# A hybrid stick-breaking and convolution layer on one core: token layout, meta scores as wide products, and spaced steps for packed values

## The chip, the core and the metric

The kernel runs on one core of a Trainium2 chip. The metric is the device time of one execution, in microseconds (us), the median over several runs. The kernel before takes 1317.13 us, the median of 3 runs from 1316.32 to 1318.55.

## What is computed

One layer over a sequence of 2048 tokens of width 1024, with 16 learned meta tokens put in front and dropped at the end, all in float32:

```
u = rms_norm(h, pre_g)
glu_a, glu_b, conv_gate, q, k, v, sb_gate = split(u @ w_in)        # 7 x 512 columns

c = glu_a * sigmoid(glu_b)
c = silu(layer_norm(causal_depthwise_conv(c, width 31)))
c = (c @ w_pw2 + b_pw2) * silu(conv_gate)

z = q.k / sqrt(64), 8 heads of 64, keys strictly before the query   # stick-breaking
a[t,s] = sigmoid(z[t,s]) * prod over s < j < t of (1 - sigmoid(z[t,j]))
s = (a @ v) * silu(sb_gate)

h + rms_norm(concat[c, s] @ w_out, post_g)
```

## The kernel before

**Arithmetic.** Each float32 operand of a large product is split into a high and a low part (`split`, L462; `ev_qk`, L903) and the product is made as high x high + high x low + low x high, with tiles of 128 stationary columns and up to 512 moving ones. Attention uses differences of neighbouring values: the running products of (1 - beta) of a row of queries come from one DVE scan, are turned by PE (`flip`, L1341), split by ACT and DVE, and multiplied with the value differences (`gather`, L1358).

**Stages.** The sequence is cut into 4 chunks of 512 tokens (`TC`); chunk 0 also carries the meta tokens. The input projection of chunk 0 runs alone; after that `merge` weaves, for each chunk c, three streams: the attention of chunk c (`attention`, L1285), a filler (gates, the output projection of chunk c-1, the convolution's end, and the input projection of chunk c+1: `tail`), and `meta_keys` of chunk c-1 (L1503). An attention goes through units (head, key chunk); each unit weighs four blocks of 128 queries against 512 keys (`weigh`, L1301), and its results are turned and gathered later, `LAG` = 3 gathers behind.

**Order.** The order of all instructions is fixed when the program is built, by a planner: `Engine.issue` (L180) keeps a planned time for each engine from cost functions (`pe_cost`, L223, `dve_cost`, `act_cost`, `pool_cost`), `Later` (L143) holds small jobs with a due time until their inputs are ready by plan, and `merge` picks the stream whose next piece is ready, with `SHARES` (L77) saying how much filler work should be done at a given amount of attention work. On the chip each engine runs its list in order and waits on semaphores. SP issues most transfers, POOL some.

**PSUM.** Eight banks in four rings (`BANKS`, L51): two for the wide products ("mm"), four for everything that is turned or weighed ("T"), one for the attention's sums ("av"), one for the convolution ("cv"). A request for a T tile takes the oldest of the four and waits until its last reader is done.

**Tokens.** `load_first_in` (L653) brings chunk 0's tokens as eight tiles of 128 features x 512 tokens from `xturn`, which lies in memory as [128 features, 8 tiles, 512 tokens]. PE starts on a tile as soon as ACT and DVE have scaled and split it (`part_in`, L864). `load_later` (L777) brings the later chunks from `xlater`, two tiles at a time.

**Meta scores.** Every query also meets the 16 meta keys. `meta_scores` (L937) runs once for each chunk and each pair of heads: for each block of 128 queries it loads the queries as stationary operand and multiplies with `km`, high queries with 64 columns (high keys, low keys) and low queries with 32 (high keys). Two DVE operations add the parts into `sgm`, of which there are two, one per parity of the chunk; the second shares a tile with the constants and is called `cp` in the profile. `meta_keys` scans these scores with the products that the attention left in `cm`, turns the result with PE into one T bank, takes it up in four steps (ACT the high part, DVE the low part, POOL a copy), and makes one product per pair of heads with `vm`, the packed meta values. DVE adds the attention's sum to that product and multiplies with the gate; ACT and POOL split the result into `mixs` for the output projection.

**Values.** `values` (L1010) projects the values, POOL takes the differences of neighbours, and `turn` (L1042), a `Later` job, turns them with PE (tile `ev`), splits them and stores them for the attention.

## Time and profile before

| | us |
|---|---|
| median of 3 runs | 1317.13 |
| the profiled execution | 1318.35 |
| its span, first to last instruction | 1316.6 |
| PE busy | 1292.9 |
| DVE busy | 1023.1 |
| ACT busy | 734.8 |
| POOL busy | 674.9 |

PE (matmuls) is busy almost throughout; its weight loads (PEld) overlap the matmuls. Matmuls overlap each other too: one of 512 columns lasts 0.4 us from start to end, and the next starts 0.23 us after it. What an instruction takes from PE is therefore read from the starts in the order of time, not from the busy column. A wait is idle time in front of an instruction, put down to what ended it.

### The profile page before, as it was taken

Reading aid. Unit: us, or ns where it says so; the run is one execution under the profiler, and the core shown is the slowest. Engines: PE = TensorE matmul, PEld = TensorE weight load, DVE = VectorE, ACT = ScalarE, POOL = GpSimd, SP = SyncE. Lnnn points to the kernel's source line nnn. Section 1 sums busy time; section 2 is a strip of 40 time slices with the busy share of each in tenths; the row PEclk is TensorE's granted clock in tenths of the full one; section 3 lists DMA queues with packets and bytes.
Section 4 is the critical chain, followed back from the end, with each engine's and each line's share of the span. In section 5 each row is a group of like instructions: output and inputs, shape, how many; then the busy total and the mean of one; then the engine's idle time right before and its main releaser. Section 6 shows DMA issues by size and latency. Waiting matters only on the chain.

```text
span 1316.6 us, 22042 instructions
## 1 busy us (share of the span) xinstructions
PE 1292.9 (98%) x7522; PEld 1115.8 (85%) x7522; DVE 1023.1 (78%) x1470; ACT 734.8 (56%) x1461; POOL 674.9 (51%) x807
## 2 busy tenths in 40 slices
PE   8999999999999999999999999999999999999897
PEld 8998888887799878887789988888787889888797
DVE  5999889998884588984587478985448987899964
ACT  6544355344465452676555544588775665666543
POOL 2555578767677430788742231499787212322402
PEclk9999999999999999999999999999999999999999
DMA  6687787999878996676756696666667456676555
GB/s 230 217 266 234 240 274 258 304 342 321 267 241 269 314 299 196 204 233 215 229 180 193 188 342 198 195 193 215 200 185 231 137 156 191 193 250 217 177 160 184
DMA packets 166399, 300.82 MB, mean 228 GB/s; under 512 B 17280, under 2 KB 71744, under 8 KB 166288
## 3 DMA queue, kind: packets, MB, share of 16 engines
q1 hardware_dynamic: 152496, 251.44, 61.5%
q0 software_dynamic: 13792, 47.98, 9.5%
q8 instruction: 59, 0.97, 0.3%
q14 instruction: 52, 0.43, 0.1%
HBM read 221.90 MB, written 77.46 MB: 227 GB/s over the span
## 4 chain that ended last, share of the span: by engine, by line
PE 86%; DVE 6%; DMA 3%; ACT 2%; issue 1%; POOL 1%; SPq 0%; DVEq 0%; POOLq 0%; ACTq 0%
PE mm L218 56%; PE T L218 21%; PE av L218 9%; DVE pr L218 1%; DMA w<-wscr 1%; DMA ev<-x 1%; DVE ul L218 1%; DVE tok L218 1%; DVE cv L218 1%; DMA tok<-xlater 1%; POOL ev L218 1%; DVE mixs L218 1%; DMA pr<-xturn 0%; DVE al L218 0%; PE cv L218 0%
## 5 line engine op out<-in xcount | busy, mean ns | idle before, releaser
L218 PE MATMUL mm<-uh,w 128*128 128x512 f32 (+1 forms) x1936 | 566.9, 379 | 1.8 <-ACT uh L218 1.5
L218 PEld LDWEIGHTS mm<-uh,w 128*128 128x128 f32 x1936 | 338.7, 190 | 54.2 <-ACT uh L218 2.2
L218 PE MATMUL mm<-ul,w 128*128 128x512 f32 (+1 forms) x968 | 358.9, 372 | 0.0
L218 DVE TENSOR_TENSOR_SCAN pr<-T,pr,zcol 128x512 f32<-128x512 f32 x192 | 245.2, 1277 | 56.6 <-ACT T L218 54.0
L218 DVE TENSOR_TENSOR al<-T,ah 128x512 fp32r<-128x512 f32 (+1 forms) x320 | 191.3, 598 | 102.9 <-ACT ah L218 101.4
L218 ACT ACTIVATE ah<-T 128x512 fp32r<-128x512 f32 (+1 forms) x320 | 170.1, 532 | 156.1 <-PE T L218 155.0
L218 DVE SCALAR_TENSOR_TENSOR cv<-ct,cp,cv 128x512 f32<-128x512 f32 x319 | 238.9, 749 | 6.7
L218 ACT ACTIVATE T<-T 128x512 f32<-128x512 f32 (+2 forms) x320 | 167.5, 525 | 109.6 <-PE T L218 103.8
L218 POOL TENSOR_TENSOR acc<-acc,pd 128x512 f32<-128x512 f32 x150 | 194.7, 1298 | 41.3 <-ACT pd L218 34.6
L218 POOL TENSOR_TENSOR w<-wr,w 128x512 fp32r<-128x512 f32 x132 | 171.3, 1301 | 80.3 <-ACT w L218 79.4
L218 PEld LDWEIGHTS mm<-ul,w 128*128 128x128 f32 x968 | 183.0, 190 | 33.9 <-DVE ul L218 0.7
L218 PE MATMUL T<-kk,q 128*128 128x512 f32 (+3 forms) x640 | 191.8, 383 | 3.4 <-DVE mixs L218 1.1
L218 PE MATMUL T<-ident,pr 128*128 128x128 f32 x1088 | 171.4, 273 | 2.7 <-DVE al L218 1.7
L218 PEld LDWEIGHTS T<-ident,pr 128*128 128x128 f32 x1088 | 135.0, 140 | 35.6 <-DVE al L218 2.7
L218 DVE TENSOR_TENSOR_SCAN pr<-T,tri 128x128 f32<-128x128 f32 (+3 forms) x128 | 103.4, 814 | 28.0 <-ACT T L218 27.8
L218 PEld LDWEIGHTS T<-kk,q 128*128 128x128 f32 x640 | 105.6, 190 | 17.5 <-issue 1.5
L218 PE MATMUL av<-ah,vk 128*128 128x512 f32 (+1 forms) x320 | 119.5, 373 | 0.0
L218 ACT ACTIVATE pd<-ct,cp 128x512 f32<-128x512 f32 x150 | 106.7, 718 | 22.7 <-POOL acc L218 21.9
L218 PE MATMUL av<-al,vk 128*128 128x512 f32 (+1 forms) x320 | 117.2, 366 | 0.0
L218 ACT ACTIVATE w<-wr 128x512 fp32r<-128x512 f32 x140 | 86.9, 626 | 38.5 <-PE mm L218 11.8
L218 POOL COPY cm<-pr 128x1 f32<-128x1 f32 x120 | 23.9, 200 | 135.1 <-DVE pr L218 134.7
L218 PE MATMUL mm<-w,mixc 128*128 128x256 f32 x600 | 80.7, 283 | 0.3 <-ACT tok L218 0.3
(212 smaller groups left out, 1574.8 us busy)
## 6 DMA issues: line engine op xcount, KB each, us to landing
w<-wscr SPq DMA_DIRECT2D x150, 512.0 KB, 4.1
wr<-wpack SPq DMA_DIRECT2D x140, 256.0 KB, 4.5
wscr<-w POOLq DMA_DIRECT2D x68, 512.0 KB, 4.8
kk<-kscr SPq DMA_DIRECT2D x80, 256.0 KB, 4.5
vk<-vscr SPq DMA_DIRECT2D x80, 256.0 KB, 3.8
q<-qscr SPq DMA_DIRECT2D x64, 256.0 KB, 5.5
vscr<-mixs SPq DMA_DIRECT2D x32, 256.0 KB, 3.5
qscr<-ehl SPq DMA_DIRECT2D x32, 256.0 KB, 3.1
```

The costliest lines, as they stand in the source:

```text
L218: return call(out, *args, **kw)
```

## The change

- `xturn` is laid out tile by tile, [8 tiles, 128 features, 512 tokens], and `xlater` in pairs of tiles, [chunk, pair, feature, 2, tokens].
- `meta_scores` takes the keys as stationary operand: 64 columns (low keys beside high keys, then high keys beside zeros) against 512 moving queries, two products for each chunk and pair of heads. ACT copies one half of the result and DVE adds the other; the four pairs of heads lie in one tile `zt` of 128 partitions x 512 queries, which takes the second `sgm`'s place. In unit 2 of the chunk's attention PE turns `zt` in four transposes, and one DVE copy brings it into `sgm`, of which there is one.
- `turn` jobs get 2.0 us on their due time.
- In `meta_keys` each value product of the first kind (all heads of a chunk) is planned at least 1.8 us after the stream came to it, the sum goes from PSUM into `sr`, and the multiplication with the gate moves from DVE to POOL.
- In `attention` a block is always weighed before the next gather; before, the last gather of a diagonal unit went ahead.
- The planner's least price for a product rises from 0.06 to 0.11, and `SHARES` moves by 1.3 to 1.9.

```
-    [(28.1, 169.2)], [(71.5, 214.4)], [(114.3, 214.4)], [(123.8, 97.4), (158.7, 126.3)],
+    [(29.8, 169.2)], [(73.1, 214.4)], [(116.0, 214.4)], [(125.1, 97.4), (160.4, 126.3)],
...
-        return t
+        return t + self.late
...
-    return (0.108 if name == "transpose" else max(n * 4.537e-4, 0.06)), 0.19
+    return (0.108 if name == "transpose" else max(n * 4.537e-4, 0.11)), 0.19
...
-    both = const.tile([P, ncp + NTB * NH * MS], F32, name="cp")
-    cp = both[:, : ncp + KD * NM]
+    both = const.tile([P, ncp + TC], F32, name="cp")
+    cp, zt = both[:, : ncp + KD * NM], both[:, ncp:]
...
-    km = const.tile([P, 2, NJ, 2 * NM], F32R, name="km")
+    km = const.tile([P, NJ, 3, 2 * NM], F32R, name="km")
...
-            sp.dma_start(ts[k], xturn[:, k])
+            sp.dma_start(ts[k], xturn[k])
...
-            sp.dma_start(t[:, k : k + 2], xlater[c - 1, :, k0 : k0 + 2])
+            sp.dma_start(t[:, k : k + 2], xlater[c - 1, k0 // 2])
...
-    def meta_scores(c, j, hi, lo):
-
-        sg = sgm[c % 2]
-        if j == 0:
-            pool.memset(sg[:, :, :, NM:], 0.0)
-        pt = PT("T", [P, TC])[:, : NTB * 4 * NM].rearrange("p (b i s) -> p b i s", b=NTB, i=2)
-        for r in range(NTB):
-            ts = slice(NM + r * P, NM + (r + 1) * P)
-            pe.matmul(pt[:, r], hi[:, ts], km[:, :, j, :], start=(r == 0), stop=False)
+    def meta_scores(j, hi, lo):
+
+        pt = PT("T", [P, TC])
+        for i, t in ((0, hi), (1, lo)):
             pe.matmul(
-                pt[:, r, 0], lo[:, ts], km[:, 0, j, :], start=False, stop=(r == NTB - 1)
-            )
-        a, b = (pt[:, :, i].rearrange("p b (e s) -> p b e s", e=2) for i in range(2))
-        dve.tensor_copy(sg[:, :, 2 * j : 2 * j + 2, 0:NM], b)
-        dve.tensor_tensor(
-            sg[:, :, 2 * j : 2 * j + 2, 0:NM], a, sg[:, :, 2 * j : 2 * j + 2, 0:NM], op=ALU.add
-        )
-        if j == NJ - 1:
-            keep["sgm", c] = True
+                pt[: 4 * NM], km[:, j, i : i + 2].rearrange("p i s -> p (i s)"), t[:, NM:],
+                start=(i == 0), stop=(i == 1),
+            )
+        zj = zt[2 * j * NM : 2 * (j + 1) * NM]
+        act.activation(zj, pt[: 2 * NM], AF.Copy)
+        dve.tensor_tensor(zj, pt[2 * NM : 4 * NM], zj, op=ALU.add)
...
-                when(lambda: turn(dv, j, P, NM, NTB), [dv], [f"v{j}"], tag="T")
+                when(lambda: turn(dv, j, P, NM, NTB), [dv], [f"v{j}"], tag="T", late=2.0)
...
-                ready = len(pend) >= LAG
-                short = ready and pend[0][0]["diag"] and pend[0][1] == NTB - 1
-                for what in (1, 0) if short else (0, 1):
-                    if what == 0 and u:
-                        yield need(heads[u["h"]]["q2"], u["kk"], tag="T")
-                        weigh(u, b)
-                    if what and ready:
-                        yield needs_of(*pend[0])
-                        gather(*pend.pop(0))
+                if u:
+                    yield need(heads[u["h"]]["q2"], u["kk"], tag="T")
+                    weigh(u, b)
+                if len(pend) >= LAG:
+                    yield needs_of(*pend[0])
+                    gather(*pend.pop(0))
...
-            if i == 1:
+            if i == 2:
+                force(zt)
+                yield need(zt, tag="T")
+                pt = PT("T", [P, NTB, NH, NM])
+                for r in range(NTB):
+                    pe.transpose(
+                        pt[:, r].rearrange("p h s -> p (h s)"), zt[:, r * P : (r + 1) * P], ident
+                    )
+                dve.tensor_copy(sgm[:, :, :, 0:NM], pt)
+                pool.memset(sgm[:, :, :, NM:], 0.0)
+                keep["sgm", c] = True
...
-            yield need(m, vm, sr, gt, tag="T")
+            ready, t0 = need(m, vm, sr, gt, tag="T"), pe.now + 1.8
+            yield lambda: ready() if part else max(ready(), t0)
             pj = PT("T", [P, TC])
             pe.matmul(pj, vm[: 6 * NM, j], m[: 6 * NM], start=True, stop=True)
             hold.difference_update((sr.name, gt.name, m.name))
-            dve.tensor_tensor(pj, pj, sr, op=ALU.add)
-            dve.tensor_tensor(sr, pj, gt, op=ALU.mult)
+            dve.tensor_tensor(pj if part else sr, pj, sr, op=ALU.add)
+            (dve if part else pool).tensor_tensor(sr, pj if part else sr, gt, op=ALU.mult)
```

## Rows read from the trace of the kernel before

**Rows 1.** The page, part 1: busy time of each engine, its share of the span and its instructions.

```profile
PE 1292.9 (98%) x7522; PEld 1115.8 (85%) x7522; DVE 1023.1 (78%) x1470; ACT 734.8 (56%) x1461; POOL 674.9 (51%) x807
```

**Rows 2.** Stretches of the span: from and to, its length, then busy us (and instructions) of PE, PEld, DVE, ACT and POOL, the granted clock, the DMA engines' busy share and GB/s.

```profile
40.00:135.00 95.00, 93.79 (x680) 88.46 (x679) 88.35 (x138) 47.33 (x98) 49.61 (x51) 1.00 0.72 231
135.00:340.00 205.00, 204.27 (x998) 168.50 (x997) 188.06 (x289) 96.00 (x192) 145.61 (x189) 1.00 0.88 294
340.00:640.00 300.00, 296.75 (x1657) 253.47 (x1656) 206.85 (x300) 167.93 (x332) 181.02 (x205) 1.00 0.76 243
640.00:985.00 345.00, 342.65 (x1920) 291.04 (x1919) 242.83 (x329) 211.04 (x408) 188.60 (x206) 1.00 0.68 212
985.00:1230.00 245.00, 242.67 (x1490) 210.26 (x1489) 216.18 (x283) 151.88 (x313) 77.21 (x104) 0.99 0.64 199
1230.00:1250.00 20.00, 16.44 (x92) 12.96 (x91) 18.33 (x28) 11.42 (x22) 9.98 (x11) 0.91 0.43 143
```

**Rows 3.** Waits of PE, longest sum first: who waited for whom, us in total, times, the longest.

```profile
PE T L218 <- DVE mixs L218: 3.7, 3, 1.7
PE T L218 <- POOL ev L218: 2.2, 3, 1.3
```

**Rows 4.** The instructions that read the tile `km`: duration in ns (least, median, most), first and last start, forms (stationary, moving).

```profile
L218 PEld LDWEIGHTS T<-km,ehl x128: 186/192/192, 118.9 to 987.5; 128*128 128x128 f32 x128
L218 PE MATMUL T<-km,ehl x128: 192/263/298, 119.1 to 987.5; 128*128 128x64 f32 x64, 128*128 128x32 f32 x64
```

**Rows 5.** PE in order of time around the first group of meta scores: start, us to the end of the last, count, and idle time before it in brackets.

```profile
118.42 0.63 PE L218 MATMUL mm<-uh,w 128*128 128x512 f32 x2
118.88 0.40 PE L218 MATMUL mm<-ul,w 128*128 128x512 f32 x1
...
119.93 0.71 PE L218 MATMUL mm<-uh,w 128*128 128x512 f32 x2
```

**Rows 6.** PE in order of time: the turned weights of the first `meta_keys` and what follows, and where PE stops in each of the three stages.

```profile
346.31 0.60 PE L218 MATMUL T<-ident,ev 128*128 128x128 f32 x4
346.67 0.71 PE L218 MATMUL T<-kk,q 128*128 128x512 f32 x2
...
353.59 0.70 PE L218 MATMUL T<-kk,q 128*128 128x512 f32 x2 [1.14 <-DVE mixs L218]
...
654.16 0.52 PE L218 MATMUL T<-ident,pr 128*128 128x128 f32 x3 [0.86 <-DVE mixs L218]
...
1001.62 0.47 PE L218 MATMUL T<-mixs,vm 96*128 96x512 f32 x1 [1.73 <-DVE mixs L218]
```

**Rows 7.** Groups of instructions by line, engine, operation, tile and shape: busy us, mean ns of one, idle time before them and what ended it. The score operations, the four-step uptake of ACT and DVE, and the product with the gate on DVE beside the nearest one on POOL.

```profile
L218 DVE TENSOR_TENSOR sgm<-T,sgm 128x128 f32<-128x128 f32 x8 | 2.3, 292 | 0.3
...
L218 ACT ACTIVATE mixs<-T 32x512 fp32r<-32x512 f32 x12 | 7.1, 590 | 10.3 <-DVE mixs L218 9.2 <-PE T L218 1.1
...
L218 DVE TENSOR_TENSOR mixs<-T,mixs 32x512 fp32r<-32x512 f32 x12 | 8.2, 685 | 6.0 <-ACT mixs L218 5.9
...
L218 DVE TENSOR_TENSOR tok<-T,tok 128x512 f32<-128x512 f32 x12 | 8.3, 691 | 0.4
...
L218 POOL TENSOR_TENSOR mixs<-tok,mixs 128x512 fp32r<-128x512 f32 x12 | 15.4, 1289 | 1.0 <-ACT mixs L218 0.9
```

**Rows 8.** PE in order of time: the longest wait in front of a value turn.

```profile
601.17 0.66 PE L218 MATMUL T<-ident,ev 128*128 128x128 f32 x4 [1.25 <-POOL ev L218]
```

**Rows 9.** DVE in order of time: the first and the fourth of the four steps of the third stage.

```profile
996.76 0.68 DVE L218 TENSOR_TENSOR mixs<-T,mixs 32x512 fp32r<-32x512 f32 x1
...
1000.78 0.69 DVE L218 TENSOR_TENSOR mixs<-T,mixs 32x512 fp32r<-32x512 f32 x1 [0.66 <-ACT mixs L218]
```

**Rows 10.** Two stretches after the third stop, columns as in rows 2.

```profile
1000.00:1005.00 5.00, 2.91 (x10) 2.20 (x11) 3.83 (x7) 3.50 (x7) 4.16 (x6) 0.87 0.17 67
1005.00:1010.00 5.00, 5.00 (x19) 3.89 (x19) 4.86 (x9) 1.50 (x3) 4.98 (x6) 0.79 0.39 111
```

**Rows 11.** The scans over the tile `sgm`, columns as in rows 4.

```profile
L218 DVE TENSOR_TENSOR_SCAN sgm<-sgm,cm x8: 408/414/1465, 341.4 to 991.1; 128x136 f32<-128x136 f32 x8
```

**Rows 12.** The tile `mixs` from 356 to 382 us: output products, POOL's low parts, and the last three value products; columns as in rows 4.

```profile
L218 PE MATMUL mm<-w,mixs x12: 278/280/363, 380.0 to 381.4; 128*128 128x256 f32 x12
...
L218 POOL TENSOR_TENSOR mixs<-tok,mixs x4: 1287/1288/1307, 360.4 to 366.7; 128x512 fp32r<-128x512 f32 x4
...
L218 PE MATMUL T<-mixs,vm x3: 391/393/399, 357.2 to 359.0; 96*128 96x512 f32 x3
```

**Rows 13.** PE in order of time at the start: the two waits for tokens.

```profile
7.93 0.76 PE L218 MATMUL mm<-uh,w 128*128 128x264 f32 x4 [0.76 <-ACT uh L218]
...
9.96 0.92 PE L218 MATMUL mm<-uh,w 128*128 128x264 f32 x4 [0.73 <-ACT uh L218]
```

**Rows 14.** Stretches of the start, columns as in rows 2.

```profile
4.00:5.00 1.00, 1.00 (x6) 1.00 (x6) 0.63 (x3) 0.60 (x3) 0.00 (x0) 1.00 0.48 113
...
8.00:9.00 1.00, 0.97 (x6) 0.75 (x6) 0.82 (x2) 0.63 (x1) 0.00 (x0) 1.00 1.02 379
...
10.00:14.00 4.00, 4.00 (x19) 3.82 (x20) 4.00 (x7) 3.95 (x7) 0.00 (x0) 0.57 1.05 404
```

**Rows 15.** PE in order of time: the longest wait between 1230 and 1250 us.

```profile
1235.20 0.66 PE L218 MATMUL T<-ident,pr 128*128 128x128 f32 x4 [1.09 <-DVE al L218]
```

**Rows 16.** The sum over three stretches, 340 to 380, 640 to 690 and 985 to 1030 us, in which the meta values are made: their length and the busy us of each engine.

```profile
sum 135.00, PE 129.82 PEld 107.65 DVE 115.60 ACT 76.28 POOL 88.28; mean PE 43.27 PEld 35.88 DVE 38.53 ACT 25.43 POOL 29.43
```

More of the change, by code (lines that the diff above doesn't have):

```diff
@@ L141, with __init__ @@
     count = 0
-    def __init__(self, clock, what, ins, outs, engine, date, room):
+    def __init__(self, clock, what, ins, outs, engine, date, room, late):
         self.clock, self.what, self.ins, self.outs = clock, what, ins, outs
-        self.engine, self.date, self.room = engine, date, room
+        self.engine, self.date, self.room, self.late = engine, date, room, late
         Later.count += 1
@@ L282, in force, with when @@
             run(clock.writers(mark)[0])
-    def when(what, ins, outs=(), engine=None, date=0.0, tag=None):
-        soon.append(Later(clock, what, ins, outs, engine, date, tag))
+    def when(what, ins, outs=(), engine=None, date=0.0, tag=None, late=0.0):
+        soon.append(Later(clock, what, ins, outs, engine, date, tag, late))
     pe = Engine(clock, nc.tensor, pe_cost, 0.15, run)
@@ L385, in trunk @@
     vl = const.tile([P, 2, P], F32R, name="vl")
-    km = const.tile([P, 2, NJ, 2 * NM], F32R, name="km")
+    km = const.tile([P, NJ, 3, 2 * NM], F32R, name="km")
     cm = const.tile([P, NTB, NH, MS], F32, name="cm")
-    sgm = [
-        const.tile([P, NTB, NH, MS], F32, name="sgm"),
-        both[:, ncp:].rearrange("p (b h s) -> p b h s", b=NTB, h=NH),
-    ]
+    sgm = const.tile([P, NTB, NH, MS], F32, name="sgm")
     ct = [const.tile([P, HIST + TC], F32, name=f"ct{j}") for j in range(NJ)]
@@ L400, in clear @@
         nc.gpsimd.memset(cm, 0.0)
+        nc.gpsimd.memset(sgm, 0.0)
     kscr = dr.tile([NH, 2, HD, NM + SEQ], F32, name="kscr")
@@ L932, in qk_proj @@
                 when(
-                    lambda a=(c, j, hi, lo): meta_scores(*a), [hi, lo], [sgm[c % 2]], tag="T",
-                    date=pe.now + 3.0,
-                )
-    def meta_scores(c, j, hi, lo):
-        sg = sgm[c % 2]
-        if j == 0:
-            pool.memset(sg[:, :, :, NM:], 0.0)
-        pt = PT("T", [P, TC])[:, : NTB * 4 * NM].rearrange("p (b i s) -> p b i s", b=NTB, i=2)
-        for r in range(NTB):
-            ts = slice(NM + r * P, NM + (r + 1) * P)
-            pe.matmul(pt[:, r], hi[:, ts], km[:, :, j, :], start=(r == 0), stop=False)
+                    lambda a=(j, hi, lo): meta_scores(*a), [hi, lo], [zt], tag="T",
+                    date=pe.now + 4.0,
+                )
+    def meta_scores(j, hi, lo):
+        pt = PT("T", [P, TC])
+        for i, t in ((0, hi), (1, lo)):
             pe.matmul(
-                pt[:, r, 0], lo[:, ts], km[:, 0, j, :], start=False, stop=(r == NTB - 1)
-            )
-        a, b = (pt[:, :, i].rearrange("p b (e s) -> p b e s", e=2) for i in range(2))
-        dve.tensor_copy(sg[:, :, 2 * j : 2 * j + 2, 0:NM], b)
-        dve.tensor_tensor(
-            sg[:, :, 2 * j : 2 * j + 2, 0:NM], a, sg[:, :, 2 * j : 2 * j + 2, 0:NM], op=ALU.add
-        )
-        if j == NJ - 1:
-            keep["sgm", c] = True
+                pt[: 4 * NM], km[:, j, i : i + 2].rearrange("p i s -> p (i s)"), t[:, NM:],
+                start=(i == 0), stop=(i == 1),
+            )
+        zj = zt[2 * j * NM : 2 * (j + 1) * NM]
+        act.activation(zj, pt[: 2 * NM], AF.Copy)
+        dve.tensor_tensor(zj, pt[2 * NM : 4 * NM], zj, op=ALU.add)
     def in_proj(c):
@@ L1037, in differences @@
                 pool.tensor_copy(vcol[c % 2][:, j], vt[:, NM + P :: P])
-                when(lambda: turn(dv, j, P, NM, NTB), [dv], [f"v{j}"], tag="T")
+                when(lambda: turn(dv, j, P, NM, NTB), [dv], [f"v{j}"], tag="T", late=2.0)
                 if c == 0:
-                    when(lambda: turn(dv, j, NM, 0, 1), [dv], [f"v{j}"], tag="T")
+                    when(lambda: turn(dv, j, NM, 0, 1), [dv], [f"v{j}"], tag="T", late=2.0)
             def turn(dv, j, rows, t0, nb):
@@ L1075, in meta_k @@
                 sp.dma_start(
-                    km[rows, i, :, e * NM : (e + 1) * NM].bitcast(F32),
+                    km[rows, :, 1 - i, e * NM : (e + 1) * NM].bitcast(F32),
                     kscr[e::2, i, :, 0:NM].rearrange("j d s -> d j s"),
@@ L1326, in weigh @@
                 bm = keep["bm"][:, h - EARLY, r, h]
-                zm = sgm[c % 2][:, r, h, 0:NM]
+                zm = sgm[:, r, h, 0:NM]
                 when(
@@ L1522, in meta_keys @@
             dve.tensor_tensor_scan(
-                fl(sg), fl(sg), fl(cm), 0.0, op0=ALU.mult, op1=ALU.max
+                fl(sgm), fl(sgm), fl(cm), 0.0, op0=ALU.mult, op1=ALU.max
             )
-        when(lambda: pool.tensor_copy(bm[:, :, hs], zm), [sg], [bm])
+        when(lambda: pool.tensor_copy(bm[:, :, hs], zm), [sgm], [bm])
         given = {}
@@ L1927, in last_room @@
         pool.memset(a[:, 4:6], 0.0)
-        zm = sgm[c % 2][:, :, EARLY:, 0:NM]
+        zm = sgm[:, :, EARLY:, 0:NM]
         act.activation(zm, zm, AF.Sigmoid, scale=-SCALE)
@@ L2008 @@
         "xturn": np.ascontiguousarray(
-            f["x"][0, :TC].reshape(TC, KD, P).transpose(2, 1, 0)
+            f["x"][0, :TC].reshape(TC, KD, P).transpose(1, 2, 0)
         ),
         "xlater": np.ascontiguousarray(
-            f["x"][0, TC:].reshape(NCH - 1, TC, KD, P).transpose(0, 3, 2, 1)
+            f["x"][0, TC:].reshape(NCH - 1, TC, KD // 2, 2, P).transpose(0, 2, 4, 3, 1)
         ),
```

3 lines of the change are left out of this document (1 added, 2 removed).

## The prediction

> **What bounds the kernel now.** I read the page first: TensorE's matmul row is busy for 1292.9 of 1316.6 us [rows 1]. Then the same by stage [rows 2]: between 40 and 1230 us PE is idle for 1.21 + 0.73 + 3.25 + 2.35 + 2.33 = 9.9 us in all, and 3.6 more between 1230 and 1250; what is left lies at the start and the end. So in the body two things count: the matmuls that PE has to issue, and the few waits that make up the 9.9 us. Work that moves between the other engines counts only where PE ends up waiting for it. Last I read whom PE waits for [rows 3]: no wait is a habit; the longest sums are 2 to 4 us, in three places each.
>
> The profiled execution took 1318.35 us (its span is 1316.6), 1.2 us over the median of the three runs, 1317.13. I make the sum against 1318.35 and take the 1.2 us off at the end. A measurement of this kernel tells about 0.2% (2.6 us) from no change.
>
> **Part 1, the meta scores.** Now each of 16 (chunk, head pair) groups issues eight products, half of 64 and half of 32 columns, each with 128 queries loaded as the stationary operand [rows 4]. In the order of time [rows 5] the last full product before a group starts at 118.88 and the first after it at 119.93; a full 512-column product takes 0.23 (two in 0.46, from 118.42 to 118.88). So a group costs 1.05 - 0.23 = 0.82 us, and 16 cost 13.1. The busy column does not give this, since pipelined products overlap. After: two 512-column products per group, 16 x 2 x 0.23 = 7.4 us, and four transposes per chunk to turn the scores back. Four transposes take 0.36 (346.31 to 346.67 in [rows 6]), 4 x 0.36 = 1.4. Saving 13.1 - 8.8 = **4.3 us**. A stationary tile of 64 columns is in no row. One end: its load hides behind the product before, as loads here do, 4.3. Other end: the whole 0.19 of a load [rows 4] lies open 32 times, 6.1 us, and the part loses 1.8. I take the first: the nearest row, the product with 96 stationary rows, takes 0.39 from start to end [rows 12], as a full one does (0.40 in [rows 5]). Off PE, two DVE operations of 0.29 per group become one ACT copy (0.59) and one DVE add (0.69), priced by the 32x512 rows of [rows 7], plus one DVE copy of a bank per chunk, some 0.7: ACT +9.4 us, DVE +4.5 us over the run. The score bank is held some 0.7 us longer, and PE is who asks for the next one; but where the first groups lie PE goes on without a gap [rows 5], so I cost it at nothing. If that cover goes, it is 16 x 0.7 = 11 us at the very most. One score buffer replaces two; it is written in unit 2 of an attention, and the previous chunk's scores are read at that attention's beginning, so no wait.
>
> **Part 2, the delayed value turns.** `turn` gets 2.0 us more on the planner's date. Its transposes are what PE waits for at POOL: 2.2 us in 3 waits, none over 1.3 [rows 3], the longest at 601.17 [rows 8]. 2.0 covers the longest, so I take **2.2 us**. Bounds: 0 (POOL is late by something else in the new order) to 2.7 (each wait also loses the overlap of a product with the next, 0.40 - 0.23). The results go to memory and are read a stage later; nothing is late next.
>
> **Part 3, the spaced steps of the meta values.** PE stops in all three stages where they lie: 1.14 at 353.59, 0.86 at 654.16, 1.73 at 1001.62 [rows 6], and after the last the granted clock falls: 0.87 and 0.79 over 5 us each, with 2.4 GHz on one side and 1.2 on the other, 1.7 us of full speed [rows 10]. What it waits for is one PSUM bank. The transposed weights (346.31 in the first stage) are taken up from it in four steps, ACT then DVE, one after another: DVE starts its first at 996.76 and its fourth at 1000.78, a step every 1.34 us, done at 1001.47 [rows 9]. PE's fourth request for a T bank after the transposes comes round to this bank, and it stops until 0.15 us after that end. The change does not shorten this chain. It puts 1.8 us before each value product, so fewer requests fall into those 5 to 7 us; only in the third stage are two of the four requests value products. So I count half of that stage's 1.73 + 1.7: **1.5 us** (1.7 would be the half; some of the main stream moves up). Bounds: 2 us lost (the main stream asks earlier and stops longer) to 1.14 + 0.86 + 1.73 + 1.7 = 5.4 gained. The second multiplication moves from DVE (12 x 0.69) to POOL, where such a product takes 1.29 [rows 7]: 15.5 us more on POOL, 8.3 less on DVE. POOL then delivers the mixed values later, by the spaced steps (7.2 us for four; now the last three start within 1.8) and one or two queued products, some 6 us in all. In the first stage the last POOL product starts at 366.7 and takes 1.29, and the output products first read its kind at 380.0 [rows 12]. The 12 us between hide it.
>
> Here a rule speaks against the change. What the trace shows first: a DVE scan with two SBUF inputs takes 1.465 us at worst against 0.414 [rows 11]. The Trainium skill, "SBUF — State Buffer", section "SBUF: two separate sides", says that a DVE operation with two SBUF inputs and a GpSimd operation exclude each other for a whole instruction. By that rule the 12 moved products can stop 12 DVE operations; this is rival (d), worked out there from the rows.
>
> **Part 4, the token layout.** PE's first products wait for tokens: 0.76 and 0.73 [rows 13], and the clock falls behind that (0.57 from 10 to 14 us, 1.7 us of full speed). From 4 to 5 us the transfers move 113 GB/s, later 379 to 404 [rows 14]. If the slow stretch came from the 16 KB pitch of the tokens' rows, up to 0.76 + 0.73 + 1.7 = 3.2 us could go. But the same pitch is moving at 379 GB/s from 8 to 9 us, while tiles 2 and 3 come in. So I take **0.5**, bounds 0 to 3.2. The Trainium skill, "DMA: Bandwidth & Descriptors", section "Latency and other measured facts", lists row pitches at large powers of two as slow, from 512 KiB on, and advises contiguous tiles; by it the whole 3.2 would come and the sum would be 1305.9. The row at 8 us does not bear that out. The later tokens' transfers hide: PE's waits have none of them.
>
> **Part 5, the planner.** Its price for a short product rises from 0.06 to 0.11, the end of a diagonal is no longer gathered before the next unit is weighed, and the shares move by 1.7. This takes no instruction away, but all orders after about 110 us are dealt anew. Waits not named above are 9.9 - 2.2 - 3.7 = 4.0 us in the body and the 3.6 at 1230 to 1250, behind DVE like the 1.09 in [rows 15]. They may shrink by half or double in the body: I take 0, between -4 and +5.
>
> **Sum.** 4.3 + 2.2 + 1.5 + 0.5 = 8.5 us; 1318.35 - 8.5 = 1309.8, less 1.2 for the median: **1308.6 us**.
>
> **Rivals.** (a) *Only the instructions go.* The new order has as many waits as the old: 1317.1 - 4.3 = 1312.8. For it: the bank chain of part 3 is untouched. Against: the waits of part 2 have a known lateness. 22%. (b) *More heals*: the start (2.7 more) and half of the waits at 1230 to 1250 (1.8): about 1304. 11%. (c) *The 64-column load lies open*: 6.1 lost, 1314.7, so the scores do not gain what they should. Every load in these rows hides. 8%. (d) *Slower: POOL locks DVE out.* In the three stages of part 3 the moved products fall on DVE operations with two SBUF inputs; each stops one by 1.465 - 0.414 = 1.05 us, 12 x 1.05 = 12.6 us; if PE waits for all of them, 1308.6 + 12.6 = 1321. It decides once DVE runs out of slack there. It has 135.0 - 115.6 = 19 us in the three [rows 16], and the move frees 8.3 more, which speaks against it; for it, that PE's stops there are already behind DVE. 12%.
>
> **How the numbers follow.** The forecast has 47%, from 1305 to 1312. Below 1302 would need (b) and more; above 1317.5 lies most of (d) and little else. Both ends together leave out about 2 in 10, so the range is 1302 to 1317.5. Faster by over 0.2% (under 1314.5): the forecast's 47, 16 of (a), (b)'s 11 and 1 of (c), together 75. Slower by over 0.2% (over 1319.8): (d), 11 of its 12. Within 0.2%: 14, the rest of (a), (c) and (d).
>
> **What would show it.** Right: 32 products of 512 columns from the packed keys, 0.46 us per group; no PE wait for POOL's differences; the four-step chain still at 1.34 us a step, with PE's stop shorter or gone in the third stage; the start within 1 us of now. Wrong: start transfers at 350 GB/s from 4 us on and PE 2 to 3 us earlier (part 4 too low); stops behind T banks or DVE of over 10 us in the body (part 5); DVE scans of 1.4 us around the moved products (d); a gap at each 64-column load (c).

## The result and the profile after

The changed kernel takes **1310.43 us** (median of 4 runs, 1310.05 to 1311.82) against 1316.99 for the kernel before in the same session: ratio 0.995, 95% interval 0.9933 to 0.9968. The profiled execution took 1310.28 us, 8.07 less than the one before (1318.35), which lay 1.2 us above its median; by the medians the gain is 6.6 us.

The page's first part and the stages answer to [rows 1] and [rows 2].

```profile
PE 1284.4 (98%) x7442; PEld 1106.4 (85%) x7442; DVE 1019.2 (78%) x1446; ACT 743.0 (57%) x1477; POOL 690.4 (53%) x820
```

```profile
340.00:640.00 300.00, 296.11 (x1638) 252.12 (x1639) 207.50 (x298) 169.81 (x337) 189.67 (x213) 1.00 0.77 245
640.00:985.00 345.00, 343.97 (x1917) 292.13 (x1916) 244.43 (x326) 217.59 (x419) 200.30 (x215) 1.00 0.69 218
985.00:1230.00 245.00, 240.33 (x1480) 208.61 (x1480) 213.26 (x279) 149.07 (x307) 77.83 (x105) 0.99 0.63 195
```

PE is busy 8.5 us less, but it does not stand still less: between 340 and 1230 us it is idle for 3.89 + 1.03 + 4.67 = 9.6 us, against 7.9 in [rows 2]. The third stop of part 3 has moved from 1001 to 990 us; the stages are cut at fixed times, so work also moves across their edges.

The busy column overlaps products, so I also add up by starts. Each product gets a slot: 0.454 ns per moving column, at least 0.108 us, and 0.1085 for a transpose. The sum of the slots is PE's **work**; what the distance from one start to the next has beyond its slot is **excess** (waits, slow clock). In all kernels here work + excess + 10.4 to 11.1 us is the profiled time. Before: 1270.5 + 37.3. After: 1265.8 + 33.6. So 4.65 of the 8.07 us are fewer slots, and 3.7 are less excess. The slots are a model: from start to start, the 16 groups with their transposes take 4.2 us less. And one trace is one execution: beside run 1 the kernel before took from 1313.7 to 1322.4 us, so a us or two of excess between two traces is not yet a difference.

**The scores.** The products over the tile `km` [rows 4], and PE in order of time around one group [rows 5]:

```profile
L218 PEld LDWEIGHTS T<-ehl,km x32: 133/134/137, 117.2 to 978.2; 128*64 128x64 f32 x32
L218 PE MATMUL T<-ehl,km x32: 387/394/478, 117.4 to 978.4; 128*64 128x512 f32 x32
```

```profile
136.06 0.39 PE L218 MATMUL mm<-ul,w 128*128 128x512 f32 x1
136.29 0.62 PE L218 MATMUL T<-ehl,km 128*64 128x512 f32 x2
136.76 0.63 PE L218 MATMUL mm<-uh,w 128*128 128x512 f32 x2
```

A group takes 136.76 - 136.29 = 0.47 us, where it took 0.82. The load of 64 columns takes 134 ns, less than the 192 of 128 columns, and hides: the next product starts 0.23 us after the one before it.

**Whom PE waits for** [rows 3], and the stops in order of time [rows 6]:

```profile
PE T L218 <- DVE pr L218: 5.3, 6, 2.0
PE T L218 <- DVE mixs L218: 4.2, 3, 2.5
```

```profile
340.88 0.68 PE L218 MATMUL T<-ehl,km 128*64 128x512 f32 x2 [1.96 <-DVE pr L218]
...
349.77 0.47 PE L218 MATMUL T<-mixs,vm 96*128 96x512 f32 x1 [0.82 <-DVE mixs L218]
350.99 0.73 PE L218 MATMUL T<-kk,q 128*128 128x512 f32 x2 [0.75 <-DVE pr L218]
...
648.02 0.52 PE L218 MATMUL T<-ident,pr 128*128 128x128 f32 x3 [0.89 <-DVE mixs L218]
...
990.80 0.47 PE L218 MATMUL T<-mixs,vm 96*128 96x512 f32 x1 [2.46 <-DVE mixs L218]
```

No wait for POOL's differences (`ev`) is left. The three stops of the meta values are all there, the third longer than before (2.46 against 1.73). New in this size is a stop of 1.96 us in front of a score product: a T bank that the attention still holds (DVE's scan `pr`). Before, the longest of that kind was 0.56 us.

DVE comes late to that scan, because it first runs the four scans of `meta_keys` from 338.15 us on. The first of them, beside a split on POOL, takes 1.37 us where the others take 0.41. The difference, 0.96 us, is by estimate half of the stop. The tile `sgm` from 338 to 341 us, then POOL in order of time:

```profile
L218 DVE TENSOR_TENSOR_SCAN sgm<-sgm,cm x4: 408/409/1372, 338.1 to 340.1; 128x136 f32<-128x136 f32 x4
```

```profile
337.93 1.29 POOL L218 TENSOR_TENSOR w<-wr,w 128x512 fp32r<-128x512 f32 x1 [1.17 <-ACT w L218]
```

DVE in order of time in the third stage, the first and the fourth step [rows 9], and the granted clock behind the stop [rows 10]:

```profile
985.95 0.68 DVE L218 TENSOR_TENSOR mixs<-T,mixs 32x512 fp32r<-32x512 f32 x1
...
989.96 0.69 DVE L218 TENSOR_TENSOR mixs<-T,mixs 32x512 fp32r<-32x512 f32 x1 [0.66 <-ACT mixs L218]
```

```profile
990.00:995.00 5.00, 4.20 (x14) 3.37 (x15) 4.51 (x7) 3.87 (x8) 4.90 (x6) 0.73 0.13 27
995.00:1000.00 5.00, 5.00 (x22) 4.01 (x21) 3.04 (x4) 1.22 (x2) 5.00 (x5) 0.93 0.39 132
```

Still (989.96 - 985.95) / 3 = 1.34 us a step, PE goes on 0.15 us after the fourth, and the clock falls as it did: 5 x (0.27 + 0.07) = 1.7 us of full speed.

**The start** [rows 14]:

```profile
4.00:5.00 1.00, 1.00 (x7) 1.00 (x6) 0.63 (x3) 0.32 (x2) 0.40 (x1) 1.00 0.95 303
...
10.00:14.00 4.00, 4.00 (x35) 4.00 (x34) 4.00 (x7) 3.38 (x6) 0.00 (x0) 1.00 1.05 412
```

303 GB/s where 113 were, and no slow clock from 10 to 14 us. The excess up to 40 us is 5.9 us, before 7.3.

### The profile page after: what moved, and what is told of

It is laid out like the page before. It is cut to its first block, busy times and chain, and to the rows that moved or that the text cites. A ratio compares the mean times of both kernels' runs of the same rounds, so it can differ in the third digit from the quotient of the medians.

```text
span 1308.5 us, 21884 instructions
## 1 busy us (share of the span) xinstructions
PE 1284.4 (98%) x7442; PEld 1106.4 (85%) x7442; DVE 1019.2 (78%) x1446; ACT 743.0 (57%) x1477; POOL 690.4 (53%) x820
## 4 chain that ended last, share of the span: by engine, by line
PE 87%; DVE 5%; ACT 2%; DMA 2%; issue 2%; POOL 1%; SPq 1%; DVEq 0%; POOLq 0%; ACTq 0%
PE mm L218 57%; PE T L218 20%; PE av L218 9%; DVE pr L218 2%; DVE ul L218 1%; ACT ev L218 1%; DMA w<-wscr 1%; DVE sgm L218 1%; DMA wr<-wpack 1%; DVE tok L218 1%; SPq L218 1%; DVE mixs L218 0%; DMA qscr<-ehl 0%; POOL w L218 0%; PE cv L218 0%
## 5 line engine op out<-in xcount | busy, mean ns | idle before, releaser
L218 PEld LDWEIGHTS mm<-ul,w 128*128 128x128 f32 x968 | 181.6, 188 | 33.6 <-DVE ul L218 0.5
L218 POOL TENSOR_TENSOR ev<-ev 64x512 f32<-64x512 f32 (+2 forms) x46 | 55.5, 1206 | 68.8 <-ACT ev L218 38.5
```

The costliest lines, as they stand in the source:

```text
L218: return call(out, *args, **kw)
```

## The experiments

Two questions were open: why the total came out nearly as forecast while one of its terms (part 3) did not come, and what the new order is worth. The theory from the two traces, A: the slots saved are real, the rest depends on how the planner's order happens to fall on busy T banks (a "deal" below: any edit deals it anew), and the four-step chain is a cost of its own that the change leaves alone. The main rival, B: each part has its own worth, the steps and the new price above all, and these add up. The expectations say what each makes of a run. Each part was done alone on the kernel before (runs 1 to 5); the changed kernel was re-dealt with no other edit (6), and three parts were undone in it (7 to 9); then the chain was taken away (10 to 12). All times stand beside the kernel before on the same chip, 1317.1 to 1317.2 us there. The last two columns are of one execution each; that one lay 3.3 us above its run's median in run 9, and within 1.6 us of it in the other runs.

| run | kernel | median us | ratio to before, 95% | PE's work | excess |
|---|---|---|---|---|---|
| | before (profile) | | 1 | 1270.5 | 37.3 |
| | after (profile) | 1310.43 | 0.995 [0.9933, 0.9968] | 1265.8 | 33.6 |
| 1 | before + token layout | 1315.83 | 0.9995 [0.9985, 1.0005] | 1270.5 | 33.6 |
| 2 | before + scores | 1319.09 | 1.0011 [1.0000, 1.0022] | 1265.8 | 42.4 |
| 3 | before + late turns | 1315.29 | 0.9984 [0.9975, 0.9994] | 1270.5 | 32.8 |
| 4 | before + spaced steps | 1324.49 | 1.0057 [1.0042, 1.0071] | 1270.5 | 43.5 |
| 5 | before + planner | 1320.38 | 1.0020 [1.0007, 1.0033] | 1270.5 | 40.5 |
| 6 | after, re-dealt | 1314.29 | 0.9975 [0.9964, 0.9986] | 1265.8 | 39.1 |
| 7 | after - scores | 1317.21 | 0.9999 [0.9991, 1.0008] | 1270.5 | 35.3 |
| 8 | after - spaced steps | 1308.36 | 0.9931 [0.9910, 0.9951] | 1265.8 | 32.7 |
| 9 | after - planner | 1314.17 | 0.9978 [0.9966, 0.9989] | 1265.8 | 41.2 |
| 10 | after + copy out | 1306.76 | 0.9921 [0.9902, 0.9940] | 1265.8 | 30.0 |
| 11 | after + copy out - spaced steps | 1303.96 | 0.9898 [0.9885, 0.9911] | 1265.8 | 27.7 |
| 12 | before + copy out | 1313.56 | 0.9969 [0.9957, 0.9981] | 1270.5 | 33.6 |

**1. The token layout alone.**

```
-  sp.dma_start(ts[k], xturn[:, k])
+  sp.dma_start(ts[k], xturn[k])
-  sp.dma_start(t[:, k : k + 2], xlater[c - 1, :, k0 : k0 + 2])
+  sp.dma_start(t[:, k : k + 2], xlater[c - 1, k0 // 2])
```

> The kernel before with the two token layouts alone. The planner does not know layouts, so every engine's list is that of the kernel before. Theory A (the layout frees the start): the first value products move up and the clock does not fall between 10 and 14 us, the start gains about 1.4 us (what the changed kernel shows at its 300th wide product) and the total 1.4. Theory B (the start of the changed kernel was a lucky run, pitch does not matter): transfers again at 110 to 210 GB/s from 4 to 7 us, total within 0.5 us of the kernel before. The later tokens' pairs bring nothing in either.

No difference in time that these executions can tell (0.05% less, the interval from 0.15% less to 0.05% more). Stretches of its start, and then of run 2's, which has the old layout:

```profile
4.00:5.00 1.00, 1.00 (x7) 1.00 (x6) 0.63 (x3) 0.36 (x2) 0.00 (x0) 1.00 0.46 172
5.00:6.00 1.00, 0.71 (x4) 0.31 (x2) 0.33 (x1) 0.00 (x0) 0.00 (x0) 1.00 0.96 354
```

```profile
4.00:5.00 1.00, 1.00 (x9) 0.99 (x7) 0.62 (x3) 0.42 (x2) 0.39 (x1) 1.00 0.70 217
5.00:6.00 1.00, 0.35 (x4) 0.12 (x2) 0.49 (x2) 0.72 (x1) 0.00 (x0) 1.00 0.90 309
```

172 GB/s with the new layout, 217 with the old: in this one us the 113 and 303 of the first two traces were largely the run. One us later the layouts part: from 5 to 6 us the six traces with the old layout move 190 to 309 GB/s, the eight with the new 311 to 377. The clock fell between 10 and 14 us in three of the six and in none of the eight. PE, DVE and ACT have the same order in all fourteen up to there. So the layout does free the start, as theory A has it, but for less than its 1.4 us: the excess up to 40 us is 6.5 to 8.1 us with the old layout (mean 7.1) and 5.7 to 6.8 with the new (mean 6.2), 0.9 us between the means.

**2. The scores alone** (`meta_scores`, `km`, `zt` and the transposes of unit 2 as in the changed kernel, and with them the due time of the scores, 4.0 us for 3.0, which belongs to the change too; gather order and price as before).

> The kernel before with the new meta scores alone (64 stationary columns, one score buffer, transposes in unit 2), layout, turns, steps, gather order and planner prices as before. Theory A: 0.46 us per group instead of 0.82 and 1.4 us of transposes, 4.3 us less of PE; the waits in front of the score products for banks that DVE has not read grow from 0.9 to 2 or 3 us, so the total gains 2 to 4 us. Theory B (the new order deals its waits at random): the total lies anywhere within 4 us of -4.3, with stops at places that have nothing to do with the scores.

4.65 us less work and not faster, so both theories missed: no gain of 2 to 4 us, and a total outside 4 us of -4.3. The excess rose from 37.3 to 42.4. Its longest new stop in PE's order of time, and the sum of PE's waits that it belongs to:

```profile
210.23 0.44 PE L218 MATMUL T<-kk,q 128*128 128x128 f32 x2 [2.25 <-DVE pr L218]
```

```profile
PE T L218 <- DVE pr L218: 6.7, 8, 2.2
```

PE stops there for a T bank that the attention's scan has not let go, well over 100 us ahead of the first meta stage. The scan comes late because DVE is held up: a copy of 30 columns (`ct`), which takes 0.17 us in the median, takes 7.42 us, while POOL runs one operation after another, and ends 0.05 us after the last of these. In order of time, DVE and then POOL:

```profile
200.25 7.42 DVE L218 COPY ct<-ct 128x30 f32<-128x30 f32 x1
```

```profile
200.77 3.78 POOL L218 TENSOR_TENSOR mixs<-acc,mixs 128x512 fp32r<-128x512 f32 x3
...
205.08 1.30 POOL L218 TENSOR_TENSOR mixs<-acc,mixs 128x512 fp32r<-128x512 f32 x1
206.33 1.29 POOL L218 TENSOR_TENSOR w<-wr,w 128x512 fp32r<-128x512 f32 x1
```

A stop of 0.86 us at 221.58 waits for `ct` as well. The two make 3.4 of the 5.1 us by which the excess rose. In the kernel before, the longest of these copies takes 1.29 us. So what the slots saved went into waits that this order made, most of them far from the scores.

**3. The late turns alone** (`late=2.0` in `when` for both `turn` jobs).

> The kernel before with 2.0 us on the due time of the value turns alone. Theory A: PE's waits for POOL's differences (2.2 us in 3 waits) go and nothing takes their place: 2 to 3 us faster. Theory B (POOL is late by something else, or the transposes stop elsewhere): waits of the same size behind other tiles, total within 1 us of the kernel before.

2.1 us gained (interval 0.8 to 3.3), the 2.2 that the prediction had. The wait for POOL's `ev` is gone from PE's waits; the one for `mixs` grew:

```profile
PE T L218 <- DVE mixs L218: 4.8, 3, 2.2
```

**4. The spaced steps alone.**

```
-  yield need(m, vm, sr, gt, tag="T")
+  ready, t0 = need(m, vm, sr, gt, tag="T"), pe.now + 1.8
+  yield lambda: ready() if part else max(ready(), t0)
...
-  dve.tensor_tensor(pj, pj, sr, op=ALU.add)
-  dve.tensor_tensor(sr, pj, gt, op=ALU.mult)
+  dve.tensor_tensor(pj if part else sr, pj, sr, op=ALU.add)
+  (dve if part else pool).tensor_tensor(sr, pj if part else sr, gt, op=ALU.mult)
```

> The kernel before with the spaced steps of the meta values and the product on POOL alone. Theory A (one bank is held for 5 to 7 us by four alternating steps of ACT and DVE, and spacing does not shorten that): PE still stops 0.15 us after the fourth step in all three stages, 3 to 4 us in all, total within 1 us of the kernel before. Theory B (spacing is the cure): the stops go, 3 to 5 us faster. Theory C (POOL's products hold up DVE): slower by some us, with DVE scans of 1.4 us or more beside them.

7.3 us lost, which theory C alone had, but not at the steps: the stops of the three stages are as before (1.31, 0.99 and 1.90 us of excess). Stretches, and PE in order of time at one point of them:

```profile
490.00:500.00 10.00, 6.12 (x26) 3.91 (x25) 10.00 (x14) 6.12 (x12) 3.38 (x7) 0.87 0.55 150
500.00:505.00 5.00, 5.00 (x20) 4.39 (x19) 4.96 (x9) 1.44 (x3) 0.00 (x0) 0.57 0.19 49
```

```profile
499.49 0.80 PE L218 MATMUL T<-kk,q 128*128 128x256 f32 x2 [2.68 <-DVE pr L218]
```

Some 130 us after the first stage DVE is busy for all of 490 to 500 us and PE for 6.1, waiting for the attention's scans, and the clock falls behind it. The edit has no instruction there; the planner has dealt that stretch anew. Why it came out so isn't settled. Theory C's cause is not it: no DVE instruction that runs beside one of POOL's 12 products is over 0.15 us longer than the median of its kind.

**5. The planner's part alone** (the price 0.11, the shares, which move by 1.3 to 1.7, and the gather of a diagonal's end in its normal turn).

> The kernel before with the planner's part alone: the price of a short product from 0.06 to 0.11, the shares moved by 1.7, and the end of a diagonal gathered in the normal turn. No instruction goes. Theory A (an order re-dealt without a saving moves the time by a few us either way, by where the stops fall): between 1314 and 1320, with the sum of PE's waits above 0.15 us within 4 us of the 37.3 of the kernel before, but at other places. Theory B (the truer price is what carried the rest of the gain, since the scores alone gave none): 1311 to 1313, with the waits 4 to 6 us less.

2.6 us slower (interval 0.9 to 4.3): the truer price carries no gain by itself, and the time lies just above theory A's range. New stops of 1.3 to 1.6 us end at 197.7, 304.5 and 950.8 us, behind `acc` and the differences `ev`.

**6. The changed kernel, re-dealt.** One number of the planner, no instruction:

```
-  return (0.108 if name == "transpose" else max(n * 4.537e-4, 0.11)), 0.19
+  return (0.112 if name == "transpose" else max(n * 4.537e-4, 0.11)), 0.19
```

> The changed kernel with one number of the planner changed, the price of a 128-column transpose from 0.108 to 0.112 us; no instruction is added or taken away. Theory A (the order is a deal; any small edit re-deals it, and a few us either way come with it): another time, by 1 to 6 us, than the changed kernel's 1310.4, more likely above; PE's excess over its modelled work 2 us or more off 33.6, the work itself 1265.8 as before. Theory B (the order is robust, and what the single edits gained or lost was their own): within 1 us of 1310.4, with the stops where they were.

0.25% slower than the changed kernel (0.9975 against 0.995; the two intervals only just touch, at 0.9964 and 0.9968), with the same work and over 5 us more excess in the profile. A price that is 4% off moves the time by about half of what the whole change gained.

**7. The changed kernel with the scores as before.**

> The changed kernel with the meta scores as before (eight short products per group); all other parts stay. Theory A (the 4.7 us of PE work are saved, and most of it shows once the rest of the order is the new one): 1313.5 to 1316, PE's modelled work back at 1270.5 us against 1265.8, no 0.7 to 2 us stops in front of score products. Theory B (the scores are worth as little here as they were alone, because PE stops longer in front of them): 1309 to 1312.

1317.21 us: the whole gain is gone, 6.5 us by the ratios, more than the 4.65 of work and above theory A's range. Alone they gave nothing (run 2), in company they give all of it: each figure holds the worth of a new order too.

**8. The changed kernel without the spaced steps** (the diff of run 4 undone).

> The changed kernel with the four steps of the meta values as they were: no 1.8 us between the value products, and DVE, not GpSimd, does the second product. Alone, on the kernel before, this part cost 7.3 us. Theory A (the steps are no gain in themselves, their loss alone was one bad deal of the order): 1307 to 1312, with PE's stops at the three stages together 6 to 8 us, as in both kernels. Theory B (the steps cost by themselves, and other parts made up for it): 1303 or less. Theory C (the steps pay once the others are there, DVE 8 us freer): 1313 or more, with more waits for DVE.

0.9931 against 0.995, intervals overlapping: the steps bring nothing that shows, and may cost 2.5 us. The third stop is the same without them, behind the same four steps:

```profile
990.51 0.58 PE L218 MATMUL T<-mixs,vm 96*128 96x512 f32 x1 [2.50 <-DVE mixs L218]
```

**9. The changed kernel with the planner's part undone.**

> The changed kernel with the planner's part undone: the old price of 0.06, the old shares, and the short gather first again. Theory A (the order is a deal that any edit re-deals): 1309 to 1316, with the excess of PE's waits 2 to 8 us over the 33.6 of the changed kernel, or as much under it, at new places. Theory B (the price and the shares fit the new score products, 0.11 per short product, and carry 4 to 6 us): 1314.5 to 1317, that is most of the gain lost.

3.7 us over the changed kernel by the ratios; the intervals just touch. That is in theory A's range and close to theory B's 4 to 6 us, so this time does not part the two; run 6, where only a price changed, speaks for A. The profile has 7.6 us more excess, in an execution 3.3 us above the run's median. Its longest stop comes right after the first stage's transposes (PE in order of time, and DVE's fourth step there). The changed kernel loses 3.5 us in three stops at that place. Run 9 also waits 1.9 us for a transfer of weights at 722 us.

```profile
338.97 0.60 PE L218 MATMUL T<-ident,ev 128*128 128x128 f32 x4
339.74 1.58 PE L218 MATMUL T<-kk,q 128*128 128x512 f32 x4 [0.17 <-DMA kk<-kscr]
341.30 0.66 PE L218 MATMUL T<-ident,pr 128*128 128x128 f32 x4
346.57 1.19 PE L218 MATMUL T<-kk,q 128*128 128x512 f32 x2 [4.61 <-DVE mixs L218]
```

```profile
345.73 0.69 DVE L218 TENSOR_TENSOR mixs<-T,mixs 32x512 fp32r<-32x512 f32 x1 [0.66 <-ACT mixs L218]
```

The transposes take a bank at 338.97; two pairs of score products (`T<-kk,q`) and one turn take the other three, with no wide product between; the fourth request comes round to the held bank and waits until 0.15 us after the step's end at 346.42. So what an order loses here depends on how soon it asks four times.

**10. The copy out.** In `meta_keys` of the changed kernel, ahead of the four steps:

```
+  if not part:
+      flat = ev()[:, :TC]
+      act.activation(flat, pt, AF.Copy)
+      pt = flat
```

> The changed kernel, and one ACT copy more per stage: the transposed weights go from the PSUM bank to an SBUF buffer before the four steps, so the bank comes free after one copy of about 0.6 us and the steps read SBUF. Theory A (ACT and DVE take turns on one PSUM bank, 1.34 us a step, and PE's fourth request for a bank falls on it): the step shrinks to 1.0 us or less, PE's stops at 349 to 351 (0.82 and 0.75), 646 (0.89) and 990 (2.46) go, and the clock does not fall at 992 to 995 (1.5 us); 1304 to 1308, which is 2 to 6 us under the changed kernel. Theory B (PE waits there because DVE and ACT have too much work at these places, bank or not): the stops stay within 1 us of what they are, behind other tiles, and the time is 1310 +- 2. Theory C (the re-dealt order decides): the stops go, but as much comes back elsewhere, 1310 or above.

1306.76 us. What the chain was shows in ACT's order of time in the changed kernel, at the first three of its four steps in the first stage:

```profile
343.42 0.59 ACT L218 ACTIVATE mixs<-T 32x512 fp32r<-32x512 f32 x1 [1.24 <-PE T L218]
345.62 0.59 ACT L218 ACTIVATE mixs<-T 32x512 fp32r<-32x512 f32 x1 [1.61 <-DVE mixs L218]
346.96 0.59 ACT L218 ACTIVATE mixs<-T 32x512 fp32r<-32x512 f32 x1 [0.75 <-DVE mixs L218]
```

ACT's second step waits for DVE's first, though it needs none of its data: each step has 32 rows of the bank of its own, both engines only read them, and the built program still has a semaphore between them. With the steps in SBUF there is no such wait: ACT does its four without a stop. ACT and then DVE in order of time with the copy, and the instructions on `mixs` from 341 to 350 us:

```profile
341.63 0.60 ACT L218 ACTIVATE ev<-T 128x512 f32<-128x512 f32 x1 [1.24 <-PE T L218]
342.26 2.60 ACT L218 ACTIVATE mixs<-ev 32x512 fp32r<-32x512 f32 x4
```

```profile
343.12 4.11 DVE L218 TENSOR_TENSOR mixs<-ev,mixs 32x512 fp32r<-32x512 f32 x4
```

```profile
L218 POOL CAST mixs<-mixs x4: 606/1056/1065, 343.0 to 345.6; 32x512 fp32r<-32x512 f32 x4
L218 DVE TENSOR_TENSOR mixs<-ev,mixs x4: 911/954/1068, 343.1 to 346.3; 32x512 fp32r<-32x512 f32 x4
```

The bank is free after 0.60 us, where it was held for 7.0 in the changed kernel's third stage (ACT's first step at 983.67 to DVE's last end at 990.65; 2.3 us of that pass before DVE's first step). A step takes 4.11 / 4 = 1.03 us, just over the expected 1.0. No wait for `mixs` is left among PE's T requests; at 990 us there are two shorter stops, behind the attention, and the clock stays up:

```profile
990.95 0.47 PE L218 MATMUL T<-mixs,vm 96*128 96x512 f32 x1 [0.86 <-DVE al L218]
...
992.05 0.44 PE L218 MATMUL T<-ident,pr 128*128 128x128 f32 x2 [0.63 <-DVE pr L218]
```

```profile
990.00:995.00 5.00, 3.50 (x15) 2.46 (x15) 4.97 (x8) 2.08 (x4) 4.98 (x5) 1.00 0.43 135
```

The time is in theory A's range; the interval still touches the changed kernel's, and the order moved too, so runs 11 and 12 test the copy under two other orders.

**11. The copy out, and no spaced steps.**

> The changed kernel with the copy of the transposed weights to SBUF and without the spaced steps (DVE does the second product at once, no 1.8 us). Theory A (once the bank is let go at once, spacing has nothing left to avoid): 1305 to 1308, as with the copy alone (1306.8) or 1 to 2 us under it, as the changed kernel without the steps was; none of PE's waits at 345 to 350, 643 to 650 and 985 to 995 above 1 us. Theory B (DVE now has both operations of each step, four times 0.69 us more in a row, and other T banks wait for it): 1309 or more, with stops behind DVE at these places.

1303.96 us (4 runs, 1303.94 to 1304.12), ratio 0.9898: the fastest of all, below theory A's range, 13 us under the kernel before and, by the ratios, 6.8 under the changed one. Against run 8, whose edit differs by the copy alone, it is 4.3 us by the ratios. Work 1265.8, excess 27.7. The longest waits of PE:

```profile
PE T L218 <- DVE pr L218: 5.1, 7, 1.1
PE T L218 <- DVE al L218: 2.0, 2, 1.1
```

No wait for the steps is left. Three stops of 1.0 to 1.15 us remain, behind the attention, one of them at 340 us and two after 1220; in the stretches that the expectation names the longest is 0.88.

**12. The copy out on the kernel before.**

> The kernel before with the copy of the transposed weights to SBUF alone. Theory A (the chain on one bank costs 3.7 us of stops and 1.7 us of clock in the kernel before as well): 1312 to 1315, steps of 1.0 us or less, and PE's stops at 353, 654 and 1001 gone. Theory B (the gain with the copy in the changed kernel was a lucky deal): 1316 to 1320, though the three stops are gone.

4.1 us gained (interval 2.5 to 5.7): with 3.8 us in run 10 and 4.3 between runs 8 and 11, the copy pays in all three pairs, so it is not one lucky deal. In its first two stages PE does not stop at all from 345 to 365 and from 645 to 665 us. In the third the bank is free, but PE stops behind the attention instead, and the clock falls (0.95 and 0.71 from 995 to 1000 and from 1000 to 1005 us):

```profile
999.26 1.01 PE L218 MATMUL T<-kk,q 128*128 128x512 f32 x2 [1.87 <-DVE al L218]
```

## Why the prediction was right, and where it was not

The time was right: 1308.6 forecast, 1310.4 measured, within the forecast case's own 1305 to 1312. Its sum was 8.5 us; the profiled execution gained 8.07, the medians 6.6. That the sum came so near is luck in part: the terms below miss by -2.0 and -1.95 one way and by 0.35, 1.1, 0.9 and 1.2 the other. Term by term, in the two traces:

| term | forecast | found |
|---|---|---|
| 1 scores, slots | 4.3 | 4.65 (4.2 from start to start) |
| 1 scores, T bank held longer | 0 | 0 |
| 2 turns | 2.2 | 3.3 with the lost overlap and two shorter waits |
| 3 spaced steps | 1.5 | -0.45 |
| 4 token layout | 0.5 | 1.4 in this pair, about 0.9 over all profiles |
| 5 in front of the score products | 0 | -2.0 |
| 5 the rest | 0 | 1.2 |

**Part 1.** The slots were sized rightly, and the first of the two ends was the right one: the 64-column load hides, so rival (c) fell. The bank that is held longer cost nothing, as forecast: no wait of PE in the changed kernel is ended by the two engines that read the scores. The reason given, "where the first groups lie PE goes on without a gap", does not hold for all groups: the excess in front of score products rose from 0.88 to 2.85 us, above all at 340.88, where the attention's scan holds the bank that the score product asks for. That is the order's, part 5. In run 2, with the same products, such waits are 2.0 us, in run 6 there are none.

**Part 2** was right in place and size: the wait for `ev` is gone in the trace and run 3 measures 2.1. With the overlap lost at each, the three waits come to 2.7 us of excess, the upper bound; two shorter ones in front of value turns, 0.3 us each, went with them.

**Part 3** failed at "so I count half of that stage's 1.73 + 1.7". That the chain stays at 1.34 us a step was right. But the chain holds the bank for 6 to 7 us, and whatever PE asks for fourth meets it: in the third stage it is again a value product, now a spaced one (990.80), that stops for 2.46 us, where 1.73 was. The excess behind `mixs` went from 4.2 to 4.66, the clock's 1.7 stayed, and run 8 shows the same stop without the spacing. The clock's part varies from run to run: run 1 has the order of the kernel before and the same stop (1.75 us), and its clock did not fall there. The 5.4 us that the prediction set as the most to be gained there is what the copy out is after: runs 10 and 12 gain 3.8 and 4.1 by the ratios.

**Part 4** was rightly kept small. The single pair of traces would have read as 1.4 us; the excess over fourteen profiles says 0.9, and run 1's time shows no difference. But the row at 8 us, from which the prediction argued that the pitch does no harm, was too late a place to look: from 5 to 6 us the layouts do differ (run 1). The rule of the Trainium skill that the prediction weighed ("DMA: Bandwidth & Descriptors", section "Latency and other measured facts", pitches at large powers of two) begins its list at 512 KiB. This pitch is 16 KB, so it did not follow from that rule that the whole 3.2 us would go, and no run here tests it.

**Part 5** stood at 0 between -4 and +5, and the bounds were about right: orders of equal work came out 3.3 us (run 6) and 3.7 us (run 9) apart from the changed kernel's. One of its signs of being wrong did show: PE's waits behind DVE between 40 and 1230 us add up to 11.7 us (6.9 before), of which 2.0 are two waits that lay beyond 1230 before. What the prediction did not see is that this part is larger than most of the others. Added up, the single parts of runs 1 to 5 would give -0.05 + 0.11 - 0.16 + 0.57 + 0.20 = +0.67%, 8.8 us slower; together they gave 0.5% faster. So the total also rests on one favourable deal. Which share of the 6.5 us of run 7 is the scores' own beyond 4.65 stays open; it would take many deals of each.

**Rival (d)** did not come where it was looked for. POOL takes 1.29 us for each moved product, as priced, and no DVE instruction beside one of the 12 is over 0.15 us longer than the median of its kind. All of these read a PSUM bank, so none with both inputs in SBUF met POOL there. What the rival describes is in both kernels all the same, beside other work of POOL, mostly splits of weights. Of the 12 scans of 136 columns (before, four of them on `cp`), three are long in either trace, 1.38 to 1.47 us before and 0.90 to 1.46 after, and one of these stands ahead of PE's stop at 340.88:

```profile
L218 DVE TENSOR_TENSOR_SCAN sgm<-sgm,cm x20: 201/408/1457, 338.1 to 1237.1; 128x136 f32<-128x136 f32 x12, 128x68 f32<-128x68 f32 x4, 128x34 f32<-128x34 f32 x4
```

**Rival (a)**, a new order with as many waits as the old, is what runs 6 and 9 show (39.1 and 41.2 us of excess); in the changed kernel's own deal it did not come.

## What to carry to other kernels

Where a planner fixes the order of everything, an edit's own saving and the re-dealt order are two things: sum PE's slots and the excess apart, and try a neighbouring deal before believing a gain or a loss of a few tenths of a per cent. Where PE's requests keep meeting one bank, look at how long its readers hold it; one copy that frees it at once was worth more than spacing the requests. A wait moved is not a wait gone: name the request that will meet the busy bank next. And where PE waits for a DVE scan, look what held DVE up: twice here it was an operation beside POOL's.

## What the runs showed of the hardware

Two engines that only read one PSUM bank went strictly by turns, 1.34 us a step, by a semaphore in the program, although ACT's next step and DVE's present one read different 32-row parts of it. The Trainium skill, "PSUM — Partial Sum Buffer", section "PSUM bank collisions raise a hardware error", says that two engines may not be at one bank within the same 32 partitions, but may be in different ones; by that the chip would not ask for this wait. No run here reads the bank without it.

With both inputs in SBUF, DVE's step took 954 ns where it took 685 from PSUM, and POOL's copies beside it 1056 ns where they took 606. That agrees with the Trainium skill, "SBUF — State Buffer", section "SBUF: two separate sides", by which such operations of DVE and GpSimd keep each other out; it is the likely reason why the step came to 1.03 us and not less, which no run takes apart.

Elsewhere, too, DVE took longer beside POOL's operations with two SBUF inputs: a scan 1.37 us for 0.41 (changed kernel, 338.15), and a copy of 30 columns 7.42 us for 0.17 (run 2, 200.25), to 0.05 us after the last of POOL's operations.

The granted clock fell behind the stops of 2.46 us (0.73 and 0.93, between the levels of 2.4 and 1.2 GHz) and 1.87 us (0.95 and 0.71), and stayed at 1.00 with two stops of 0.86 and 0.63 us. But the length of a stop does not tell: the clock also stayed at 1.00 behind the 1.96 us at 340.88, the 2.25 us of run 2 and the 1.75 us of run 1's third stage. What parts these cases is not shown here.
